# Two transposed outputs moved into PSUM banks, and two sums of the next block moved behind its first quad's sums

## The chip, the cores and the metric

The kernel runs on one core of a Trainium2 chip. The metric is the device time of one execution in microseconds (us); medians over several executions are given. Each execution also has its mean granted TensorE clock, where 1.000 is full speed. Below, PE is TensorE (matrix products), DVE is VectorE, ACT is ScalarE, POOL is GpSimd. In the timelines below ACT and DVE run their instructions in the order in which they were issued: in the kernel before, the product that the first copy reads has ended by 344.31 us, and the copy starts at 348.02, right behind the exponential issued ahead of it.

## The reference

```python
def reference(a, b):                    # a: 1024 x 4096, b: 4096 x 4096, float32
    x = np.matmul(a, b)
    return special.logsumexp(x, axis=-1).astype(np.float32)
```

## The kernel before

The kernel multiplies with a Strassen-like scheme: 2x2 blocks, seven products in place of eight. The products work in float16 and add up in float32 in PSUM. The columns of b come in eight blocks of 512, of which 3 to 6 are "wide": each is done in two halves, with seven products of 16 matmuls of 128x512 per half. Block 7 follows in four "quads", each with seven products of 16 matmuls of 128x256. The products need sums of pieces of b ("t1", "t3", "t4", "t6", "t7") which DVE makes (a "make" below is one such addition or subtraction, for a quarter of a block).

A wide half leaves four outputs c11, c12, c21, c22 in four PSUM banks. Each is transposed in 32x32 squares by DVE into a place in SBUF (c12 and c21 share one, `slots[0]`, so c21 must wait for c12's sum); then DVE takes maxima and subtracts them, ACT takes the exponential, and DVE sums (the returned function `end..`; c22 gets its maxima subtracted and its sums made within sixteen small exponentials instead). `merge_turned` merges these with the results so far: a minimum on DVE, a subtraction on POOL, an exponential on ACT.

```python
    slots = tb[:, 1, KP // 2 : KP]...      # two SBUF places, in the half of t4 that wide blocks do not use

    def lse_turned(c, slot, h, r, by_rows=False):
        nm = tnm[:, 1 + h, ts(r, WN // 2)]
        v = blocks32(slot)
        nc.vector.transpose(out=slot, in_=c)
        nc.vector.tensor_reduce(out=nm, in_=v, axis=AX.X, op=ALU.max, negate=True)
        # ... (by_rows: sixteen small exponentials, no sum left over)
        add(v, v, nm.unsqueeze(-1).broadcast_to((P, WN // 2, 32)))
        nc.scalar.activation(out=slot, in_=slot, func=AF.Exp)
        return lambda: nc.vector.tensor_reduce(
            out=tts[:, 1 + h, ts(r, WN // 2)], in_=v, axis=AX.X, op=ALU.add
        )

    # the second part of wide_step, for each half nt; last: the half before block 7
            end12 = lse_turned(c12, slots[0], 1, 0)
            end22 = lse_turned(c22, slots[1], 1, 1, True)
            product(c21, ...)
            sub(s[:, 1], c21, s[:, 1])
            end12()
            end21 = lse_turned(c21, slots[0], 0, 1)
            end22()
            # ... first half of t4 and t7 of what comes next
            product(c11, ...)
            add(c11, c11, s[:, 1])
            e = fix_pool.tile([P, FD], f32, name=f"ew_{blk.nb}_{nt}", tag="e")
            end11 = lse_turned(c11, e, 0, 0)
            end21()
            if last:
                for what in ("t4", "t7"):
                    for g in range(G // 2, G):
                        mk(what, g * GI, (g + 1) * GI)
            deferred.extend([end11, merge_turned])
```

`deferred` is issued in the next half, or in block 7's first quad, where it stands here:

```python
            m1(c11, start=True)                       # products 1 and 2
            m5(c12)
            nc.scalar.copy(out=e, in_=halves(r0))     # "first copy" on ACT
            m2(c21, start=True)                       # products 3 and 4 of the seven
            m6(c22)
            nc.scalar.copy(out=s[:, 2], in_=c21)      # "second copy"
            flush()
            add(s[:, 2], s[:, 2], e[:, 1])            # the quad's sums, on DVE
            sub(s[:, 0], s[:, 2], e[:, 0])
            for f in deferred:
                f()
            deferred.clear()
            # ...
            m3(c12)                                   # product 5
            nc.scalar.copy(out=x[:, 0], in_=c12)      # "third copy"
            m4(c21)                                   # product 6, needs t4
            nc.scalar.copy(out=x[:, 1], in_=c21)      # "fourth copy"
            m7(c11)                                   # product 7, needs t7; waits for the third copy
            sub(x, x, s[:, 0::2])
```

The prediction below miscounts by one: what it calls the fourth and the fifth product of the quad are `m3` and `m4`, the fifth and the sixth. Its last product is `m7`.

Of the kernel before, what the change touches and what calls it, by code (L numbers as in the profile page):

```python
# [13 lines left out]
def kernel(  # L14
# [7 lines left out]
    P = 128  # L22
    FD = 512
    H = FD // 2
    f32 = mybir.dt.float32
# [11 lines left out]
    GI = KP // G  # L37
# [7 lines left out]
    fix_pool = ctx.enter_context(tc.tile_pool(name="fix", bufs=1))  # L45
# [12 lines left out]
            name=nc.get_next_instruction_name(),  # L58
# [26 lines left out]
    def add(o, x, y):  # L85
        nc.vector.tensor_tensor(out=o, in0=x, in1=y, op=ALU.add)  # L86

    def sub(o, x, y):
        nc.vector.tensor_tensor(out=o, in0=x, in1=y, op=ALU.subtract)  # L89
# [262 lines left out]
    deferred = []  # L352

    def flush():
        for f in pending:
            f()
        pending.clear()
# [13 lines left out]
    slots = tb[:, 1, KP // 2 : KP].rearrange("p i n -> p (i n)").bitcast(f32)  # L371
    slots = [slots[:, 0:FD], slots[:, FD : 2 * FD]]
    blocks32 = lambda t: t.rearrange("p (c n) -> p c n", n=32)
# [6 lines that stand above are left out]
        if by_rows:  # L380
            for i in range(WN // 2):
                nc.scalar.activation(  # L382
                    out=v[:, i],
                    in_=v[:, i],
                    func=AF.Exp,
                    bias=nm[:, i : i + 1],
                    accum_out=tts[:, 1 + h, r * WN // 2 + i : r * WN // 2 + i + 1],
                )
            return lambda: None
# [5 lines that stand above are left out]
# [27 lines left out]
    def wide_step(blk, nxt):  # L422
        for nt in range(2):
            last = not nxt.wide and nt == 1

            def mk(what, lo=None, hi=None):
                if nt == 0:
                    blk.make(what, lo, hi, nt=1)
                else:
                    nxt.make(what, lo, hi)  # L430

            cs = [
                psum_pool.tile([P, FD], f32, name=f"wide_{blk.nb}_{nt}_{j}", tag="ps")
                for j in range(4)
            ]
            c11, c12, c21, c22 = cs
            s = fix_pool.tile([P, 2, FD], f32, name=f"sw_{blk.nb}_{nt}", tag="s")

            def product(c, lhs, rhs, start=False, stop=False):
                for i in range(KP):  # L440
                    nc.tensor.matmul(  # L441
                        c.rearrange("p (q m) -> p q m", m=P),
                        lhs(i),
                        rhs(i),
                        start=(start and i == 0),
                        stop=(stop and i == KP - 1),
                        skip_group_check=True,
                    )

            cols = lambda i, kp, h: blk.b(i, kp, h)[:, ts(nt, P)]  # L450
            product(c11, lambda i: blk.T1[:, i], lambda i: s1[:, i], start=True)
            product(c12, lambda i: cols(i, 1, 1), lambda i: s5[:, i], start=True)
            product(c21, lambda i: cols(i, 0, 0), lambda i: s2[:, i], start=True)
            if last:
                for what in ("t1", "t6", "t3"):
                    for g in range(G // 2, G):
                        mk(what, g * GI, (g + 1) * GI)
            nc.scalar.copy(out=s[:, 1], in_=c12)
# [4 lines that stand above are left out]
            add(s[:, 1], s[:, 1], c21)  # L463
            sub(s[:, 0], s[:, 1], c11)
            if last:
                for g in range(G // 2):
                    mk("t1", g * GI, (g + 1) * GI)
            else:
                mk("t1")
            product(c22, lambda i: blk.T6[:, i], lambda i: aT[:, i, 0, :, 1], start=True, stop=True)  # L470
            for what in ("t6", "t3"):
                if last:
                    for g in range(G // 2):
                        mk(what, g * GI, (g + 1) * GI)
                else:
                    mk(what)
            product(c12, lambda i: cols(i, 0, 1), lambda i: aT[:, i, 0, :, 0], stop=True)
            sub(s[:, 0], c12, s[:, 0])
            add(c22, c22, s[:, 0])
            end12 = lse_turned(c12, slots[0], 1, 0)  # L480
            end22 = lse_turned(c22, slots[1], 1, 1, True)
            product(c21, lambda i: blk.T4[:, i], lambda i: aT[:, i, 1, :, 1], stop=True)
            sub(s[:, 1], c21, s[:, 1])
            end12()
            end21 = lse_turned(c21, slots[0], 0, 1)
            end22()
            for what in ("t4", "t7"):
                if last:
                    for g in range(G // 2):
                        mk(what, g * GI, (g + 1) * GI)  # L490
                else:
                    mk(what)
            product(c11, lambda i: cols(i, 1, 0), lambda i: aT[:, i, 1, :, 0], stop=True)
            add(c11, c11, s[:, 1])
            e = fix_pool.tile([P, FD], f32, name=f"ew_{blk.nb}_{nt}", tag="e")
            end11 = lse_turned(c11, e, 0, 0)
            end21()
            if last:
                for what in ("t4", "t7"):
                    for g in range(G // 2, G):  # L500
                        mk(what, g * GI, (g + 1) * GI)
            deferred.extend([end11, merge_turned])

    blk, nxt = None, blk1
    for step, (_, qs) in enumerate(plan):
        blk, nxt = nxt, None
# [3 lines left out]
        if more:  # L510
            if plan[step + 1][0] is again1:
                nxt = last
            else:
                nxt = plan[step + 1][0]()
# [21 lines left out]
        if blk.wide:  # L536
            wide_step(blk, nxt)
            continue
# [4 lines left out]
        for q in qs:  # L543
# [5 lines left out]
            c11, c12 = r0[:, 0:H], r0[:, H:FD]  # L549
            c21, c22 = r1[:, 0:H], r1[:, H:FD]  # L550
# [15 lines left out]
            if final:  # L566
                c22 = psum_pool.tile([P, FD], f32, name="c22", tag="ps")[:, 0:H]
            s = fix_pool.tile([P, 4, H], f32, name=f"s_{step}_{q}", tag="s")
            x, e = s[:, 1::2], s[:, 0:2]
            if final:  # L570
                e = fix_pool.tile([P, 2, H], f32, name="e_last", tag="e")
            if joint and q > 0:
                e = e_next
# [78 lines left out]
            if final:  # L652
# [13 lines left out]
                w = s.rearrange("p a n -> p (a n)")[:, 0 : H + 1]  # L666
# [97 lines left out]
```

## Time and profile before

| what | before |
|---|---|
| median when the change was predicted, 6 runs | 421.9 us (421.49 to 423.1) |
| PE busy, profiled run | 410.5 of 420.4 us |
| clock | 1.000 |
| PE idle at the passage from the last wide half to block 7 | 0.84 + 1.00 us |

PE is busy for 98% of the span. After the start-up it stands still twice, and both times it is in block 7's first quad. The timeline of PE shows it. Its columns are start (us), duration (us), engine, line, operation, out<-in and shapes; in brackets is the idle time before, and what ended it. L621 is the first copy, L696 the third.

```profile
345.89 1.91 PE L554 MATMUL acc_0_1_3278<-tb,aT 128*128 128x256 f16 x16
348.64 0.60 PE L554 MATMUL acc_0_0_3277<-b_0_2891,aT 128*128 128x256 f16 x4 [0.84 <-ACT s_0_3279 L621]
...
350.38 1.91 PE L554 MATMUL acc_0_1_3278<-tb,aT 128*128 128x256 f16 x16
353.30 0.60 PE L554 MATMUL acc_0_0_3277<-b_0_2891,aT 128*128 128x256 f16 x4 [1.00 <-ACT s_0_3279 L696]
...
355.04 1.91 PE L554 MATMUL acc_1_0_3411<-tb,s_71 128*128 128x256 f16 x16
```

Why do these copies come late? The timeline of ACT at the same place: the first copy stands behind c11's exponential (L391), which waits for DVE; the third stands behind the merge's exponential (L405).

```profile
347.49 0.63 ACT L391 ACTIVATE ew_1_3259<-ew_1_3259 128x512 f32<-128x512 f32 x1 [3.02 <-DVE ew_1_3259 L86]
348.02 0.57 ACT L621 COPY s_0_3279<-acc_0_0_3277 128x512 f32<-128x512 f32 x1
348.49 0.38 ACT L625 COPY s_0_3279<-acc_0_1_3278 128x256 f32<-128x256 f32 x1
352.70 0.28 ACT L405 ACTIVATE ident<-ident 128x96 f32<-128x96 f32 x1 [3.84 <-POOL ident L399]
352.89 0.35 ACT L696 COPY s_0_3279<-acc_0_0_3277 128x256 f32<-128x256 f32 x1
```

And DVE, which has a backlog there. After c11's subtraction of maxima (L86 at 346.76) come c21's sum, the four makes of t4 and t7, the two quad sums, c11's sum and the merge's minimum (L401), without a gap.

```profile
346.76 0.69 DVE L86 TENSOR_TENSOR ew_1_3259<-ew_1_3259,ident 128x512 f32<-128x512 f32 x1
347.37 0.68 DVE L392 TENSOR_REDUCE tts<-tb 128x16 f32<-128x512 f32 x1
348.08 0.69 DVE L89 TENSOR_TENSOR tb<-b_2_2893 128x1024 f16<-128x1024 f16 x1
...
350.50 0.42 DVE L86 TENSOR_TENSOR s_0_3279<-s_0_3279 128x256 f32<-128x256 f32 x1
350.95 0.42 DVE L89 TENSOR_TENSOR s_0_3279<-s_0_3279 128x256 f32<-128x256 f32 x1
351.29 0.68 DVE L392 TENSOR_REDUCE tts<-ew_1_3259 128x16 f32<-128x512 f32 x1
351.89 0.25 DVE L401 TENSOR_REDUCE tmin<-ident 128x32 f32<-128x96 f32 x1
```

### The profile page before, as it was taken

Reading aid. Unit: us, or ns where it says so; the run is one execution under the profiler, and the core shown is the slowest. Engines: PE = TensorE matmul, PEld = TensorE weight load, DVE = VectorE, ACT = ScalarE, POOL = GpSimd, SP = SyncE. Lnnn points to the kernel's source line nnn. Section 1 sums busy time; section 2 is a strip of 40 time slices with the busy share of each in tenths; the row PEclk is TensorE's granted clock in tenths of the full one; section 3 lists DMA queues with packets and bytes.
Section 4 is the critical chain, followed back from the end, with each engine's and each line's share of the span. In section 5 each row is a group of like instructions: output and inputs, shape, how many; then the busy total and the mean of one; then the engine's idle time right before and its main releaser. Section 6 shows DMA issues by size and latency. Waiting matters only on the chain.

```text
span 420.4 us, 7085 instructions
## 1 busy us (share of the span) xinstructions
PE 410.5 (98%) x2747; PEld 260.4 (62%) x2747; DVE 316.4 (75%) x709; ACT 120.9 (29%) x447; POOL 91.8 (22%) x189
## 2 busy tenths in 40 slices
PE   7999999999999999999999999999999998999996
PEld 3455558888888844444444444444444477888885
DVE  2556587978647548969787896978789997299955
ACT  2222241142132210515124060514315052222124
POOL 8667753001010020013101031013100233320000
PEclk9999999999999999999999999999999999999999
DMA  9999999999999399004970099102990079499000
GB/s 184 199 202 202 203 205 207 207 207 214 184 195 184 55 178 207 16 2 68 207 127 0 2 160 207 33 1 34 207 162 2 0 119 207 76 185 207 11 2 0
DMA packets 57841, 53.28 MB, mean 127 GB/s; under 512 B 10192, under 2 KB 56912, under 8 KB 57808
## 3 DMA queue, kind: packets, MB, share of 16 engines
q0 software_dynamic: 48928, 49.95, 72.0%
q1 hardware_dynamic: 8880, 2.89, 4.2%
q8 instruction: 21, 0.34, 0.3%
q14 instruction: 12, 0.10, 0.1%
HBM read 100.66 MB, written 2.10 MB: 244 GB/s over the span
## 4 chain that ended last, share of the span: by engine, by line
PE 87%; DMA 6%; DVE 4%; issue 1%; POOL 1%; ACT 0%; POOLq 0%; DVEq 0%; ACTq 0%
DMA tb<-in_a_dram 5%; PE acc_1_0_1347 L554 2%; PE acc_1_0_767 L554 2%; PE acc_2_0_769 L554 2%; PE acc_2_0_1482 L554 2%; PE acc_0_0_765 L554 2%; PE acc_3_0_3859 L554 2%; PE acc_3_0_3723 L554 2%; PE acc_2_0_3587 L554 2%; PE acc_1_0_3411 L554 2%; PE acc_3_0_1615 L554 2%; PE acc_0_0_1215 L554 2%; PE wide_1_1_3085 L441 2%; PE wide_0_1_2900 L441 2%; PE wide_1_2_2708 L441 2%; PE wide_0_0_2521 L441 2%
## 5 line engine op out<-in xcount | busy, mean ns | idle before, releaser
L554 PEld LDWEIGHTS <-aT 128*128 128x128 f16 x832 | 81.4, 98 | 11.7 <-issue 2.2
L441 PEld LDWEIGHTS <-tb 128*128 128x128 f16 x384 | 37.6, 98 | 45.1
L382 ACT ACTIVATE tb<-tb,ident 128x32 f32<-128x32 f32 x128 | 39.1, 307 | 6.6 <-DVE ident L379 6.6
L391 ACT ACTIVATE tb<-tb 128x512 f32<-128x512 f32 x16 | 10.0, 622 | 89.6 <-DVE tb L86 89.6
L399 POOL TENSOR_TENSOR ident<-ident,tmin 128x96 f32<-128x96 f32 x8 | 3.1, 384 | 131.8 <-DVE tmin L401 131.8
L205 POOL DMA_DIRECT2D tb<-in_a_dram x47 | 25.5, 546 | 6.3 <-issue 1.4
L227 DVE COPY aT<-tps_99 128x512 f16<-128x512 f16 x24 | 10.2, 424 | 20.6 <-PE tps_99 L216 20.6
L229 ACT COPY aT<-tps_100 128x512 f16<-128x512 f16 x24 | 14.0, 585 | 39.3 <-PE tps_100 L216 39.3
L234 PEld LDWEIGHTS <-aT 128*128 128x128 f16 x192 | 16.6, 98 | 13.8 <-DVE aT L227 1.3
L382 ACT ACTIVATION_READ_ACCUMULATOR tb<-tb,ident 128x1 f32 x128 | 23.9, 187 | 0.0
L216 PEld LDWEIGHTS <-tb 128*128 128x128 f16 x192 | 14.5, 98 | 14.7 <-DMA tb<-in_a_dram 4.8
L554 PEld LDWEIGHTS <-s_71 128*128 128x128 f16 x208 | 20.3, 98 | 2.8
L554 PEld LDWEIGHTS <-s_72 128*128 128x128 f16 x208 | 20.3, 98 | 2.4
L554 PEld LDWEIGHTS <-s_73 128*128 128x128 f16 x208 | 20.3, 98 | 2.4
L379 DVE TENSOR_REDUCE ident<-tb 128x16 f32<-128x512 f32 x24 | 16.5, 686 | 1.4
L89 DVE TENSOR_TENSOR aT<-aT 128x256 f16<-128x256 f16 (+1 forms) x56 | 16.1, 339 | 0.0
L86 DVE TENSOR_TENSOR tb<-tb,ident 128x512 f32<-128x512 f32 x16 | 11.1, 692 | 0.6
L216 PE MATMUL tps_99<-ident,tb 128*128 128x128 f16 x96 | 9.5, 223 | 1.4 <-DMA tb<-in_a_dram 1.2
L392 DVE TENSOR_REDUCE tts<-tb 128x16 f32<-128x512 f32 x16 | 10.8, 677 | 0.0
L216 PE MATMUL tps_100<-ident,tb 128*128 128x128 f16 x96 | 9.3, 219 | 0.6 <-DMA tb<-in_a_dram 0.6
L86 DVE TENSOR_TENSOR s_71<-aT 128x256 f16<-128x256 f16 (+1 forms) x26 | 8.2, 314 | 1.6 <-ACT aT L229 1.5
L86 DVE TENSOR_TENSOR s_72<-aT 128x256 f16<-128x256 f16 (+1 forms) x26 | 8.2, 314 | 0.0
(907 smaller groups left out, 939.1 us busy)
## 6 DMA issues: line engine op xcount, KB each, us to landing
tb<-in_a_dram POOLq DMA_DIRECT2D x47, 128.0 KB, 5.9
aT<-in_b_dram POOLq DMA_DIRECT2D x4, 1024.0 KB, 15.1
b_1_86<-in_b_dram POOLq DMA_DIRECT2D x4, 256.0 KB, 6.4
b_2_87<-in_b_dram POOLq DMA_DIRECT2D x4, 256.0 KB, 6.2
b_3_88<-in_b_dram POOLq DMA_DIRECT2D x4, 256.0 KB, 6.2
b_0_89<-in_b_dram POOLq DMA_DIRECT2D x2, 512.0 KB, 9.3
b_1_90<-in_b_dram POOLq DMA_DIRECT2D x2, 512.0 KB, 12.5
b_2_91<-in_b_dram POOLq DMA_DIRECT2D x2, 512.0 KB, 15.4
```

The costliest lines, as they stand in the source:

```text
L86: nc.vector.tensor_tensor(out=o, in0=x, in1=y, op=ALU.add)
L89: nc.vector.tensor_tensor(out=o, in0=x, in1=y, op=ALU.subtract)
L205: nc.gpsimd.dma_start(out=slot, in_=a_m[m, :, k0 * P : (k0 + kn) * P])
L216: nc.tensor.matmul(pst[:, ts(j, P)], src[:, ts(j, P)], ident, is_transpose=True, start=(j == 0), stop=(j == kn - 1),)
L227: nc.vector.tensor_copy(out=dst, in_=v)
L229: nc.scalar.copy(out=dst, in_=v)
L234: nc.tensor.matmul(pt, aT[:, i, kp, m // 2, m % 2, :], blk0.raw[i // GI][:, i % GI, kp, :], start=(done[m] == 0), stop=(done[m] == KT - 1),)
L379: nc.vector.tensor_reduce(out=nm, in_=v, axis=AX.X, op=ALU.max, negate=True)
L382: nc.scalar.activation(out=v[:, i], in_=v[:, i], func=AF.Exp, bias=nm[:, i : i + 1], accum_out=tts[:, 1 + h, r * WN // 2 + i : r * WN // 2 ...
L392: return lambda: nc.vector.tensor_reduce(out=tts[:, 1 + h, ts(r, WN // 2)], in_=v, axis=AX.X, op=ALU.add)
L441: nc.tensor.matmul(c.rearrange("p (q m) -> p q m", m=P), lhs(i), rhs(i), start=(start and i == 0), stop=(stop and i == KP - 1), skip_group ...
L554: nc.tensor.matmul(c, lhs(i), rhs(i), start=(start and i == 0), stop=(i == KP - 1), skip_group_check=True,)
```

## The change

The intent, as far as the diff tells it: c21 and c11 go into the banks of c22 and c12, whose products have been taken out by then. So the half of t4 that held a slot is free earlier, an SBUF tile is saved, and block 7's first sums need not stand behind four makes. For the half before block 7, the second half of t4 and t7 is issued after the first quad's sums, and c21's sum after that.

```diff
-            end21 = lse_turned(c21, slots[0], 0, 1)
+            end21 = lse_turned(c21, c22, 0, 1)
             end22()
...
             add(c11, c11, s[:, 1])
-            e = fix_pool.tile([P, FD], f32, name=f"ew_{blk.nb}_{nt}", tag="e")
-            end11 = lse_turned(c11, e, 0, 0)
-            end21()
+            end11 = lse_turned(c11, c12, 0, 0)
             if last:
                 for what in ("t4", "t7"):
                     for g in range(G // 2, G):
-                        mk(what, g * GI, (g + 1) * GI)
-            deferred.extend([end11, merge_turned])
+                        deferred.append(lambda w=what, g=g: nxt.make(w, g * GI, (g + 1) * GI))
+            deferred.extend([end21, end11, merge_turned])
```

## The prediction

> **What bounds the kernel now.** TensorE: the page gives PE 410.5 us of 420.4 us (98%) at a granted clock of 0.9 or more in every slice, and the chain of waits is 87% PE. After the start-up PE stands still only twice, both at the passage from the last wide half-block to block 7 (timeline, PE): 0.84 us before the fourth product of block 7's first quad (at 348.64, released by the ACT copy of line 621) and 1.00 us before its last product (at 353.30, released by the ACT copy of line 696). Together 1.84 us. There the chain runs through DVE, which is busy almost without a gap from 333.95 to 352.1. Everywhere else DVE waits for PE (2.0 us idle at each wide half's c21), so small DVE savings there are worth nothing.
>
> **What the change does.**
> 1. Eight times, two transposes, maxima, additions, exponentials and sums move from SBUF f32 to PSUM f32. The trace has both kinds: additions 0.69 us in either; maxima 0.69 (SBUF) against 0.68 (PSUM); exponentials 0.62 (SBUF) against 0.66 (PSUM, with accumulator). The Trainium skill ("VectorE: DVE Perf Modes", the perf-mode tier table) gives f32 tensor_tensor and tensor_reduce one tier, 1x, for SBUF and PSUM alike; the durations above agree. I expect at most 0.05 us per instruction. c21's transpose no longer follows the sum that frees its slot: 0.71 us start to start becomes about 0.60, 0.1 us saved per half.
> 2. In seven of eight halves DVE's order hardly changes, and PE waits for nothing: worth 0.
> 3. At the passage, DVE's order after c11's addition (ends 347.45) is now: c21's sum (0.60), four makes of t4/t7 (2.42), block 7's two quad sums (0.8), c11's sum, merge's minimum (start 351.89). It becomes: quad sums, makes, c21's sum, c11's sum, minimum.
>
> **The critical path.** First stall: it ends with the ACT copy of line 621, queued behind c11's exponential, which waits for c11's addition on DVE. Nothing before that is removed; only the 0.1 us of point 1 helps: 0.84 becomes about 0.7.
> Second stall: PE waits for line 696, queued on ACT behind merge's exponential (352.70), which follows POOL's subtraction (352.29) and DVE's minimum (351.89). From minimum to PE: 1.41 us. In the new order the quad sums come first, but they need the ACT copy of line 625 (348.49 to 348.87), so DVE stands idle about 1.4 us from 347.45 to 348.9, where today it does useful work. Then, as an estimate from these spacings: quad sums to 349.7, makes to 352.1, two sums to 353.3, minimum at 353.3, PE released at 353.3 + 1.4 = 354.7, less 0.1. The second stall grows from 1.0 to about 2.4 us. The second half of t4 is ready (by 351.0) before the fifth product needs it (about 351.3 to 351.7).
>
> After that PE runs without a gap to the end, so the delay goes straight into the time: about +1.2 us.
>
> **Predicted: 423.1 us, 80% range 421.9 to 424.0; faster by over 2%: 0.005; within 2%: 0.985; slower by over 2%: 0.01.**
>
> **What would show it.** DVE idle 1.3 to 1.5 us before block 7's first quad sum, released by line 625; the minimum 1.2 to 1.5 us later; PE's stalls 0.7 and about 2.4 us; PSUM forms within 0.05 us of the SBUF ones; the rest of PE's timeline shifted unchanged.
>
> **What would make it wrong.** PSUM-to-PSUM transposes that are clearly faster or slower than 0.72 us; PE's last product released without the ACT copy, so that the minimum's delay is hidden; t4's second half arriving late; executions that scatter (421.49 to 423.1) as widely as the effect.

## The result, and the profile after

| | before | after |
|---|---|---|
| median | 421.57 us (20 runs, 421.07 to 423.1) | 424.39 us (10 runs, 422.79 to 425.74) |
| ratio | | 1.0058 (95%: 1.0044 to 1.0072) |
| span of the profiled run | 420.4 us | 423.1 us |
| clock of the profiled run | 1.000 | 0.996 |

A ratio is the mean time of one kernel's fast runs over that of the other's of the same rounds, so it is not quite the ratio of the two medians. The change is slower by 0.6%, and it lies outside the predicted range (421.9 to 424.0 us).

The timeline of PE after the change, same columns. L619 and L694 are the first and the third copy.

```profile
345.61 1.91 PE L552 MATMUL acc_0_1_3265<-tb,aT 128*128 128x256 f16 x16
348.32 0.60 PE L552 MATMUL acc_0_0_3264<-b_0_2884,aT 128*128 128x256 f16 x4 [0.80 <-ACT s_0_3266 L619]
...
350.06 1.91 PE L552 MATMUL acc_0_1_3265<-tb,aT 128*128 128x256 f16 x16
354.38 0.97 PE L552 MATMUL acc_0_0_3264<-b_0_2884,aT 128*128 128x256 f16 x4 [2.42 <-ACT s_0_3266 L694]
355.14 1.06 PE L552 MATMUL acc_0_0_3264<-b_1_2885,aT 128*128 128x256 f16 x4
...
357.70 2.00 PE L552 MATMUL acc_1_0_3403<-tb,s_71 128*128 128x256 f16 x16
```

The second stall is 2.42 us in place of 1.00. It ends as before with the third copy, which stands behind the merge's exponential on ACT; only both come 1.1 us later:

```profile
347.18 0.58 ACT L391 ACTIVATE wide_1_1_3077<-wide_1_1_3077 128x512 f32<-128x512 f32 x1 [3.03 <-DVE wide_1_1_3077 L86]
347.67 0.59 ACT L619 COPY s_0_3266<-acc_0_0_3264 128x512 f32<-128x512 f32 x1
353.79 0.28 ACT L405 ACTIVATE ident<-ident 128x96 f32<-128x96 f32 x1 [5.26 <-POOL ident L399]
353.98 0.35 ACT L694 COPY s_0_3266<-acc_0_0_3264 128x256 f32<-128x256 f32 x1
```

But something else is there too: the last product takes from 354.38 to 357.70, or 3.32 us, where it took 1.74 before (353.30 to 355.04). Groups of four matmuls now start 0.86 us apart, and started 0.44 us apart. The table of stretches shows why: between 354.4 and 357.8 the granted clock (after the engines' busy times) is 0.51. Its columns are the stretch, its length, the busy time and number of instructions for PE, PEld (weight loads), DVE, ACT and POOL, then the clock, the DMA share and GB/s.

```profile
352.00:354.40 2.40, 0.01 (x1) 0.01 (x1) 1.23 (x3) 0.61 (x3) 0.62 (x2) 1.00 1.25 209
354.40:357.80 3.40, 3.40 (x17) 2.44 (x17) 1.21 (x2) 0.21 (x1) 2.98 (x16) 0.51 1.24 206
357.80:361.00 3.20, 3.20 (x31) 2.84 (x30) 1.62 (x3) 0.00 (x0) 2.83 (x19) 0.99 1.16 193
```

The same place before the change has full clock:

```profile
352.00:353.30 1.30, 0.30 (x4) 0.11 (x2) 0.14 (x1) 0.59 (x3) 0.61 (x2) 1.00 1.25 210
353.30:355.00 1.70, 1.70 (x16) 1.53 (x16) 1.21 (x2) 0.22 (x1) 1.45 (x6) 1.00 1.25 209
```

The timeline of DVE after the change has the gap that was foreseen, 1.48 us before the first quad sum, released by the second copy (L623), and the minimum at 352.98:

```profile
346.38 0.70 DVE L86 TENSOR_TENSOR wide_1_1_3077<-wide_1_1_3077,ident 128x512 f32<-128x512 f32 x1
348.57 0.42 DVE L86 TENSOR_TENSOR s_0_3266<-s_0_3266 128x256 f32<-128x256 f32 x1 [1.48 <-ACT s_0_3266 L623]
349.03 0.42 DVE L89 TENSOR_TENSOR s_0_3266<-s_0_3266 128x256 f32<-128x256 f32 x1
...
352.38 0.68 DVE L392 TENSOR_REDUCE tts<-wide_1_1_3077 128x16 f32<-128x512 f32 x1
352.98 0.25 DVE L401 TENSOR_REDUCE tmin<-ident 128x32 f32<-128x96 f32 x1
```

The difference of the two profiled spans is 423.1 - 420.4 = 2.7 us, and it can be added up. The stalls grew by 0.80 + 2.42 - 0.84 - 1.00 = 1.38 us. The last product lost 3.32 - 1.74 = 1.58 us, and the next one 0.09 (1.84 against 1.75 us start to start). That makes 3.05. PE came to the passage 0.28 us earlier in this execution (340.37 against 340.65), which leaves 2.77. This arrival scatters between 339.3 and 340.8 us over the profiles, whatever the kernel; PE's first product after the start-up, near 61 us, mostly scatters with it.

The executions agree with a clock that sometimes falls. Of 11 executions of the changed kernel (the profiled one included) seven had a mean clock of 0.995 or 0.996, and their mean time is 424.7 us. Four had 0.999 or 1.000: 422.79, 422.99, 423.33 and 425.07 us. Three of these four lie where the prediction put the kernel; why the fourth is so long isn't known. (The kernel before has such an execution too, 424.43 us at full clock, in the rounds of one group of the experiments below.)

### The profile page after: what moved, and what is told of

It reads as the page before. It is cut to its first block, busy times and chain, and to the rows that moved or that the text cites. A ratio compares the mean times of both kernels' runs of the same rounds, so it can differ in the third digit from the quotient of the medians.

```text
span 423.1 us, 7100 instructions
## 1 busy us (share of the span) xinstructions
PE 412.8 (98%) x2747; PEld 261.4 (62%) x2747; DVE 316.1 (75%) x709; ACT 120.5 (28%) x447; POOL 91.8 (22%) x189
## 4 chain that ended last, share of the span: by engine, by line
PE 87%; DMA 5%; DVE 4%; POOL 2%; issue 1%; ACT 1%; POOLq 0%; ACTq 0%; DVEq 0%
DMA tb<-in_a_dram 5%; PE acc_1_0_1347 L552 2%; PE acc_1_0_767 L552 2%; PE acc_1_0_3403 L552 2%; PE acc_2_0_769 L552 2%; PE acc_2_0_3579 L552 2%; PE acc_2_0_1482 L552 2%; PE acc_0_0_765 L552 2%; PE acc_3_0_3851 L552 2%; PE acc_3_0_1615 L552 2%; PE acc_0_0_1215 L552 2%; PE acc_3_0_3715 L552 2%; PE wide_1_1_3077 L441 2%; PE wide_0_2_2894 L441 2%; PE wide_1_0_2700 L441 2%; PE wide_0_1_2517 L441 2%
## 5 line engine op out<-in xcount | busy, mean ns | idle before, releaser
L391 ACT ACTIVATE tb<-tb 128x512 f32<-128x512 f32 x8 | 5.0, 630 | 90.1 <-DVE tb L86 90.1
L379 DVE TENSOR_REDUCE ident<-tb 128x16 f32<-128x512 f32 x16 | 11.0, 686 | 1.1
L86 DVE TENSOR_TENSOR s_71<-aT 128x256 f16<-128x256 f16 (+1 forms) x26 | 8.2, 314 | 2.0 <-ACT aT L229 1.8
L86 DVE TENSOR_TENSOR s_72<-aT 128x256 f16<-128x256 f16 (+1 forms) x26 | 8.2, 315 | 0.0
L86 DVE TENSOR_TENSOR s_73<-aT 128x256 f16<-128x256 f16 (+1 forms) x26 | 8.2, 314 | 0.0
L405 ACT ACTIVATE ident<-ident 128x96 f32<-128x96 f32 x8 | 2.3, 282 | 15.4 <-POOL ident L399 15.4
```

What stands on the lines that cost most here:

```text
L86: nc.vector.tensor_tensor(out=o, in0=x, in1=y, op=ALU.add)
```

## The experiments

All kernels gave the reference's result. Each was timed in five rounds against the kernel before, on the same chip. "Lower clock" below means an execution at 0.996 or less. The kernel of before never had less than 0.998 in these rounds. Small losses of clock, 0.998 or 0.999, come from the end of the kernel: in the profiles the clock falls after PE has finished.

| run | median us | ratio to before (95%) | PE's stalls in its profile, us | lower clock |
|---|---|---|---|---|
| PSUM places only | 421.31 | 0.999 (0.9978 to 1.0002) | 0.79 + 0.83 | 0 of 5 |
| order only | 424.06 | 1.0051 (1.0031 to 1.007) | 0.83 + 2.48 | 4 of 6 |
| idle filled | 422.89 | 1.0029 (1.0016 to 1.0043) | 0.80 + (2.3 filled) + 0.26 | 0 of 5 |
| t4 made first | 420.74 | 0.9977 (0.9962 to 0.9992) | 0.80 + 0.32 | 0 of 5 |
| one instruction fewer | 423.34 | 1.0028 (1.0005 to 1.005) | 0.80 + 2.13 | 2 of 6 |
| one more | 425.57 | 1.0083 (1.0062 to 1.0103) | 0.79 + 3.14 | 6 of 6 |
| two more | 427.38 | 1.012 (1.0097 to 1.0142) | 0.80 + 3.87 | 6 of 6 |
| copies first | 420.04 | 0.9946 (0.9926 to 0.9966) | none | 0 of 6 |
| merge late | 420.28 | 0.9968 (0.9956 to 0.9981) | 0.80 + 0 | 0 of 5 |
| ACT's queue only | 419.53 | 0.9951 (0.9937 to 0.9964) | none | 0 of 5 |

The theory after the result has two parts: the new order of DVE delays the merge's minimum, and with it the ACT copy and PE, by 1.4 us; and the longer idle time makes the chip halve PE's clock for one stretch of 3.4 us (below: a window), at about 1.6 us more. The rivals: the PSUM places cost time and the order is harmless (B); the last product is slow because of what runs beside it (D).

### PSUM places only

```diff
--- before
-            end21 = lse_turned(c21, slots[0], 0, 1)
+            end21 = lse_turned(c21, c22, 0, 1)
-            e = fix_pool.tile([P, FD], f32, name=f"ew_{blk.nb}_{nt}", tag="e")
-            end11 = lse_turned(c11, e, 0, 0)
+            end11 = lse_turned(c11, c12, 0, 0)
```

> The two outputs go to the PSUM banks, but the order of before is kept (c21's sum and the second half of t4 and t7 follow c11's exponential at once). Theory A (the new order alone costs the time; the PSUM places are free): TensorE's two stalls at the passage to block 7 are 0.8 and 1.0 us as before, the clock is 1.000, time 421.4 to 421.7 us. Rival B (PSUM to PSUM work is slower, or collides with TensorE's writes): the time lies clearly above before, by 0.6 us or more, and the eight halves' DVE and ACT instructions are longer than 0.75 and 0.66 us.

Measured: 421.31 us, 0.999 of before. The interval reaches 1.0002, so a gain isn't shown, and a loss of the size in question is excluded. The median lies just under the expected 421.4 to 421.7 us. Rival B falls.

### Order only

```diff
--- after
-            end21 = lse_turned(c21, c22, 0, 1)
+            end21 = lse_turned(c21, slots[0], 0, 1)
-            end11 = lse_turned(c11, c12, 0, 0)
+            e = fix_pool.tile([P, FD], f32, name=f"ew_{blk.nb}_{nt}", tag="e")
+            end11 = lse_turned(c11, e, 0, 0)
+            deferred.append(end21)
...
-            deferred.extend([end21, end11, merge_turned])
+            deferred.extend([end11, merge_turned])
```

> The places of before (an SBUF slot for c21, an SBUF tile for c11), the order of the change; only c21's sum comes before the four makes, as they overwrite its slot, and this leaves the number of DVE instructions ahead of the merge the same. Theory A: the second stall is 2.3 to 2.5 us as after the change, the time 422.8 to 424.6 us with the clock below 1 in most executions. Rival B: the time is that of before, 421.6 us.

Measured: 424.06 us, 1.0051 of before, against 1.0058 for the whole change. The order alone costs all of it, as far as these intervals can tell. The executions fall into two groups again: four at the lower clock with 424.04 to 425.29 us, two at full clock with 422.36 and 422.94. The profiled execution is one of the latter, and its last product took its usual 1.74 us after 2.48 us of idle:

```profile
353.49 1.91 PE L554 MATMUL acc<-b,aT 128*128 128x256 f16 x16 [2.48 <-ACT s L696]
355.23 1.91 PE L554 MATMUL acc<-tb,s 128*128 128x256 f16 x16
```

So the same stall sometimes costs the clock and sometimes doesn't.

### Idle filled

```diff
--- after
             m4(c21)
+            if early and q == 0:                       # block 7's first quad
+                quads[1] = acc_tiles(f"{step}_1")      # the next quad's banks, free by now
+                for _ in range(10):
+                    nc.tensor.matmul(
+                        quads[1][0], s1[:, 0, q], blk.raw[0][:, 0, 0, :], start=True, stop=True
+                    )
             nc.scalar.copy(out=x[:, 1], in_=c21)
             m7(c11)
```

> The changed kernel, with ten matmuls of 128x512 (0.216 us each, 2.16 us in all) that nobody reads, put into the 2.4 us in which TensorE stands still. Theory C (the idle time makes the clock gate halve the clock for one window of 3.4 us, and this is the 1.6 us that the prediction lacked): the last product starts no earlier (stall plus filling 2.4 us), but its 16 matmuls take 1.75 us instead of 3.3, the clock is 1.000 in every execution, time 422.8 to 423.2 us. Rival D (the last product is slow for another reason: its operands are being made by DVE while it runs, or the loads of DMA disturb it): it takes 3.3 us again, time 424.4 us.

Measured: 422.89 us, no execution at the lower clock (order only, on the same chip in the same rounds, had four of six), and the last product took 354.72 to 356.46, or 1.74 us. The clock column reads 1.00 there (of the two executions at 0.998, the profiled one lost it at the kernel's end). Nothing else was changed: the makes, DVE's work and the loads beside the last product stayed. Rival D falls. Matmuls that nobody reads bought back 1.2 to 1.5 us (0.0029 between the two ratios to before, and 424.39 to 422.89 between medians of different rounds). What is left, 0.0029 of 421.7 us, is 1.2 us: the delay that the prediction had forecast. The timeline of PE of this run:

```profile
352.13 2.32 PE L699 MATMUL acc<-b,s 128*128 128x512 f16 x10
354.72 1.91 PE L552 MATMUL acc<-b,aT 128*128 128x256 f16 x16 [0.26 <-ACT s L694]
356.46 1.91 PE L552 MATMUL acc<-tb,s 128*128 128x256 f16 x16
```

### The length of the idle time: one instruction fewer, one more, two more

These change the number of DVE instructions between the quad's sums and the merge in the changed kernel.

```diff
--- after (for the half before block 7; the list in the order issued)
-    t4 g2, t4 g3, t7 g2, t7 g3, end21, end11, merge_turned
+    t4 g2, t4 g3, t7 g2, end21, end11, merge_turned, t7 g3            # one fewer
+    t4 g2, t4 g3, t7 g2, t7 g3, end21, end11, end11, merge_turned     # one more
+    t4 g2, t4 g3, t7 g2, t7 g3, end21, end11, end11, end11, merge_turned   # two more
```

> The changed kernel, but the last quarter of t7 is made after the merge, so one DVE instruction of 0.6 us fewer stands between the quad sums and the merge. Delay theory: the second stall is 1.8 us instead of 2.4. Clock theory (the clock record is cut into windows of 3.41 us that run on freely; a window in which TensorE stands still for more than about 1.8 us halves the clock for the next one): few or no executions at 0.995 to 0.996, time 422.3 us. If the lost 1.6 us belong to the new order and not to the idle time, the time is 423.8 us or more.

> The changed kernel with c11's sum taken twice (same result), one DVE instruction of 0.6 us more ahead of the merge. Delay theory: second stall 3.0 us. Clock theory with free windows: about four executions in five at 0.995 to 0.996, those at 425.1 us, the others at 423.5. Rival (a timer that counts from the start of the idle time, about 2.4 us): all executions at the lower clock.

> The changed kernel with c11's sum taken three times, 1.2 us more ahead of the merge: second stall 3.6 us. Both clock theories: all executions at 0.996 or below, time 425.7 us. Without any clock effect: 424.1 us.

Measured: with stalls of 2.13, 2.42 to 2.48, 3.14 and 3.87 us in the profiles, 2 of 6, 11 of 17, 6 of 6 and 6 of 6 executions had the lower clock (the second is the change and the order-only run together). The idle time is the dose, and the clock answers to it.

Three expectations missed. With one instruction fewer the stall was 2.13 us, not 1.8, and the median 423.34 us, not 422.3, with two executions at the lower clock where few or none were expected. The reason is in the timelines: POOL's subtraction of the merge took 0.70 us in place of 0.38, while the make that had been moved ran beside it on DVE. With one more, all six executions had the lower clock, where the theory of free windows said about four in five; six of six is what its rival, a timer that counts from the start of the idle time, had said. Six runs can't tell these two apart; the profiles below can. And with two more the stall was 3.87 us and the median 427.38, where 425.7 was expected. Half of the executions there, and two of six with one more, had a mean clock of 0.992. A loss of 0.008 of some 426 us is 3.4 us, the loss of two windows at half clock. Where the second one lies isn't shown, as no such execution was profiled. The limit found below doesn't explain it for one more: a stall of 3.14 us can't put more than 1.84 us into each of two windows, unless it was longer in those executions.

How much idle time does it take? The trace's clock record shows that the windows run on by themselves: after the change the low clock lasted 3.413 us, it began 102 such windows (348.16 us) after the record's first stretch at full clock did, and ended 19 windows before it fell at the kernel's end. From this grid one can place the idle times (an estimate from the clock record and the times of the matmuls). In the profiled run of the change, the 2.4 us of idle lay in one window, 351.05 to 354.46, and the clock fell. In that of the order-only run, a boundary at 352.85 cut the 2.48 us into 1.84 and 0.64, and the clock stayed. A timer with a fixed limit that counts from the start of the idle time doesn't fit these two. With one instruction fewer the profiled stall was cut into 0.99 and 1.14: the clock stayed, but it fell in two others with the same kernel, where at most 2.13 us can lie in one window if their stalls were as long. The ends of the profiles, where PE stops, give a bound without that "if": in the idle-filled run the window from 416.58 to 419.99 holds 1.18 us of PE's work, so 2.23 us of idle, and the clock falls at its end. So the limit lies between 1.84 us (clock kept) and 2.23 us (clock lost) of idle in one 3.4 us window. No window of the twelve profiles contradicts it.

### t4 made first

```diff
--- after
             if last:
-                for what in ("t4", "t7"):
-                    for g in range(G // 2, G):
-                        deferred.append(lambda w=what, g=g: nxt.make(w, g * GI, (g + 1) * GI))
-            deferred.extend([end21, end11, merge_turned])
+                for g in range(G // 2, G):
+                    mk("t4", g * GI, (g + 1) * GI)
+                # deferred: end21, end11, merge_turned, then t7's second half
```

> The changed kernel, but the second half of t4 is made at once, in the 1.5 us in which DVE waits for the quad's copies, and the second half of t7 follows the merge. The merge's minimum then starts about 2.4 us earlier, at 350.6 us. If the delay of TensorE is the DVE instructions between the quad sums and the merge, the second stall falls from 2.4 to 0.1 us or less, the first stays 0.8 us, the clock is 1.000, and the time is 420.4 to 420.9 us, below before. If TensorE waits for something else there, the stall stays at 1 us or more and the time at 421.5 or above.

Measured: 420.74 us, 0.9977 of before. The second stall is 0.32 us, not 0.1: POOL's subtraction took 0.70 us here too, beside the makes of t7. The lines of three engines show the chain from the minimum to PE:

```profile
350.50 0.25 DVE L401 TENSOR_REDUCE tmin<-ident 128x32 f32<-128x96 f32 x1
350.67 1.47 DVE L86 TENSOR_TENSOR b<-b 128x1024 f16<-128x1024 f16 x2
350.90 0.70 POOL L399 TENSOR_TENSOR ident<-ident,tmin 128x96 f32<-128x96 f32 x1 [9.15 <-DVE tmin L401]
351.63 0.28 ACT L405 ACTIVATE ident<-ident 128x96 f32<-128x96 f32 x1 [3.16 <-POOL ident L399]
351.82 0.35 ACT L703 COPY s<-acc 128x256 f32<-128x256 f32 x1
352.22 0.60 PE L561 MATMUL acc<-b,aT 128*128 128x256 f16 x4 [0.32 <-ACT s L703]
```

### The place in ACT's queue: merge late, ACT's queue only, copies first

If the cause is the place of two exponentials in ACT's queue, moving these alone must remove the stalls, with DVE's order as the change has it. (In both runs the merge's minimum is still the next DVE instruction after c11's sum.)

```diff
--- after (merge late)
-            deferred.extend([end21, end11, merge_turned])
+            deferred.extend([end21, end11])
+            (late if last else deferred).append(merge_turned)
...
             m7(c11)
+            for f in late:          # behind the third and fourth copy
+                f()
+            late.clear()
```

```diff
--- merge late (ACT's queue only)
-        nc.scalar.activation(out=slot, in_=slot, func=AF.Exp)
+        exp = lambda: nc.scalar.activation(out=slot, in_=slot, func=AF.Exp)
+        if exp_later:
+            deferred.append(exp)    # issued behind the first and second copy
+        else:
+            exp()
...
-            end11 = lse_turned(c11, c12, 0, 0)
+            end11 = lse_turned(c11, c12, 0, 0, exp_later=last)
```

"Copies first" has both edits and also another order on DVE: t4's second half at once, t7's after the quad's sums.

> The changed kernel with DVE's order kept up to c11's sum; only the merge is issued after the first quad's last two copies, so that its exponential no longer stands ahead of them on ACT. Queue theory (TensorE's second stall is the place of the merge's exponential in ACT's queue, not the number of DVE instructions as such): the second stall falls from 2.4 to 0.1 us or less, the first stays 0.8, no execution at the lower clock in the passage, time 420.6 to 421.0 us. Rival (the quad's sums or the sums t4 and t7 themselves come too late after the change): a second stall of 0.5 us or more stays.

> The run with the merge late, and c11's exponential issued after the first quad's first two copies too. DVE's instructions keep the order of the changed kernel. Queue theory: both stalls 0 to 0.2 us, time 419.7 to 420.2 us, equal to the kernel whose DVE order was changed as well. Rival (the DVE order matters too): t4's second half, made after the quad sums, comes late and TensorE waits 0.3 us or more in its fifth product.

> The changed kernel, with block 7's copies no longer behind other work on ACT: c11's exponential is issued after the first quad's first two copies, the merge after its last two; t4's second half is made at once, t7's after the quad sums. If both stalls come from the order of ACT's queue, both are gone (0 to 0.1 us each), TensorE runs through the passage, clock 1.000 there, time 419.6 to 420.0 us, 1.8 us below before and 0.8 us below the kernel with t4 made first. If a stall of 0.3 us or more stays, TensorE waits for something else.

Measured: merge late 420.28 us, the first stall 0.80 and the second gone. ACT's queue only 419.53, copies first 420.04 us, both without a stall there. The stalls are as expected; the medians lie up to 0.3 us outside the expected ranges, the first two below and the last above. The last two were timed on different chips against their own runs of before, and their intervals overlap: the order on DVE adds nothing that these runs can tell. PE and ACT with ACT's queue only:

```profile
347.07 1.91 PE L558 MATMUL acc<-b,aT 128*128 128x256 f16 x16
348.81 1.91 PE L558 MATMUL acc<-tb,aT 128*128 128x256 f16 x16
350.56 1.91 PE L558 MATMUL acc<-b,aT 128*128 128x256 f16 x16
```

```profile
344.66 0.59 ACT L625 COPY s<-acc 128x512 f32<-128x512 f32 x1 [0.80 <-DVE wide L86]
347.27 0.37 ACT L629 COPY s<-acc 128x256 f32<-128x256 f32 x1 [2.02 <-PE acc L558]
347.54 0.59 ACT L392 ACTIVATE wide<-wide 128x512 f32<-128x512 f32 x1
349.01 0.37 ACT L700 COPY s<-acc 128x256 f32<-128x256 f32 x1 [0.89 <-PE acc L558]
350.76 0.37 ACT L702 COPY s<-acc 128x256 f32<-128x256 f32 x1 [1.37 <-PE acc L558]
353.21 0.28 ACT L410 ACTIVATE ident<-ident 128x96 f32<-128x96 f32 x1 [2.08 <-POOL ident L404]
```

The first copy starts at 344.66 now, and it started at 348.02 in the kernel before, and the merge's exponential comes last, where nobody waits for it. With 0.9951 of before this kernel is, with copies first (0.9946), the fastest, and it keeps the change's places in PSUM and its order on DVE.

## Why the prediction was wrong

**The direction and the mechanism were right.** The prediction said that DVE would stand idle for 1.3 to 1.5 us before the first quad sum, released by the second copy: 1.48 us. It said that the minimum would come 1.2 to 1.5 us later; it came at 352.98 against 351.89, 1.1 later, or 1.37 later after the earlier arrival of 0.28 is allowed for. It said that the second stall would be about 2.4 us: 2.42.

**PSUM places: nearly right, and worth nothing.** Additions and maxima take 0.69 to 0.70 us in either memory, transposes 0.70 to 0.72 into SBUF and 0.72 to 0.73 into PSUM. The exponential was put at 0.66 us in PSUM, taken from a form with an accumulator; it takes 0.57 to 0.58, against 0.61 to 0.63 in SBUF. The Trainium skill ("ScalarE: Activation LUTs", the section "Step-by-step: what each stage is for") says that ACT writes to PSUM faster than to SBUF. These runs don't show that: the exponential's source moved together with its destination, and ACT's copies of 128x512 from PSUM to SBUF take 0.57 to 0.59 us too, as long as the exponential within PSUM. The 0.1 us that the earlier transpose of c21 was to save is visible (0.71 to 0.60 us start to start), but the first stall was 0.80 us rather than 0.7: from c11's subtraction of maxima to its exponential it is 0.80 us now, and was 0.73, and from its transpose to its maxima 0.77 and 0.75.

**The step that failed** is this sentence: "After that PE runs without a gap to the end, so the delay goes straight into the time: about +1.2 us", with "the rest of PE's timeline shifted unchanged". PE ran without a gap, but not at the same clock. A term of the sum was missing. In the profile the 2.42 us of idle were followed by 3.41 us at half clock, a loss of 1.67 us (1.58 in the last product, 0.09 in the next), and seven of 11 executions have the mean clock that goes with it (0.995 or 0.996). The filled idle time shows that idle is the cause: it brings back the full clock and 422.89 us, with the same delay. With that, the predicted 423.1 us is about what the kernel takes when its clock doesn't fall (three of four such executions: 422.79 to 423.33); the median belongs to the more frequent, slower group.

The page to read would have been "TensorE: Matmul & The Clock Gate" of the Trainium skill, in "Part 1: The HAM clock gate (the "warmup" mystery)": the clock falls to half after an idle window of about 3.4 us, windows run freely, and how many matmuls are slow after a cold start varies from run to run. The trace agrees on the half (0.51), on 3.413 us and on the free windows. Its rule, no idle gaps over about 3 us (section "Why this matters for your kernels"), would have passed 2.42 us as harmless; here it wasn't. Nor did the window have to be idle throughout: 0.99 us of work was in it (3.41 - 2.42).

**Scatter.** The prediction named it as a risk. It is real, and part of it has a cause that the profiles support: the phase between the windows and the stall.

## What to carry to other kernels

A stall of PE costs more than its length once it is long enough to make the clock fall (here 2.42 us of idle, and 1.67 us more), and whether it does can change from one execution to the next: look at the clock column just after every stall near 2 us, and at the clocks of all executions before comparing medians. When PE waits for an evacuation copy, look at what stands ahead of it in that engine's queue; here moving two exponentials behind the copies removed both stalls, while the change's reordering of DVE, which feeds them, lengthened one. An instruction that is issued early and must wait for another engine holds up what stands behind it, however cheap it is: here an exponential of 0.28 us.

## What the Trainium skill lacked or had wrong

- "TensorE: Matmul & The Clock Gate": the rule allows idle gaps of up to about 3 us. Here a kernel with 2.42 us of idle in its profile lost the full clock in 7 of 11 executions, and one with 2.13 us in 2 of 6. The limit is a part of the window, between 1.84 and 2.23 us idle out of 3.413 in these profiles. The page gives no such part.
- "SBUF — State Buffer", section "Who interferes with whom", says that a DVE instruction with two SBUF inputs contends with a POOL instruction that reads SBUF. It agrees, but has no size for so small an instruction: POOL's 128x96 subtraction took 0.69 to 0.70 us at the passage in the five runs in which a DVE addition or subtraction ran beside it, and 0.38 us in the seven others.
- "ScalarE: Activation LUTs" says that ACT is faster to PSUM than to SBUF. It isn't shown wrong here, but these runs give no sign of it: with the source in PSUM, a 128x512 f32 exponential into PSUM took 0.57 to 0.58 us and a copy into SBUF 0.57 to 0.59 us (two functions, so no proof). The exponential with source and destination in SBUF took 0.61 to 0.63 us.
